# Router products in pairs on the halves of PE's columns, the second chunk's rows loaded later, and other numbers of buffers

## The chip, the cores and the metric

The kernel runs on one core of one Trainium2 chip. The metric is the device time of one execution in microseconds; the engines are named PE (matrix products, with PEld for its weight loads), DVE (vector), ACT (scalar activations), POOL (GpSimd) and SP (which here only issues transfers). 1607.1 us is the median of three runs (1601.46 to 1607.68).

## The reference, cut to what matters

```
h  = rmsnorm(x, g_mix) * (1 + sc1) + sh1            # x: 2048 tokens x 1024; sh, sc, gates from silu(c) @ ada_w
u  = a * sigmoid(gt),  [a, gt] = h @ w_in + b_in     # 1024 -> 2 x 1024
y  = causal depthwise conv of u, 31 taps, + b_dw
y  = silu(layernorm(y)) @ w_out
x  = x + g1 * y                                      # called x1 in the kernel
h  = rmsnorm(x, g_ffn) * (1 + sc2) + sh2
group = argmax(h @ w_rg + b_rg) of 4; the two best of the group's 8 experts by h @ w_re + b_re
x  = x + g2 * sum over the two of gate * ((silu(h @ w_gate[e]) * (h @ w_up[e])) @ w_down[e])
out = rmsnorm(x, g_final)
```

The router's weights are 4 + 32 = 36 columns. All is float32 at the interface; the large products are made of three products of split numbers (high x high, high x low, low x high).

## The kernel before, in words

The convolution half works on four chunks of 512 tokens (`c` 0 to 3) and, in each, on eight slices of 128 channels (`j` 0 to 7). A main loop over `s = 8 c + j` (L821) writes down, for each step, `conv_in` (two products of 24 matmuls each into `pg` and `pa`, then the gate, then the store of `u`, L410), with a lag of one step `dw` (the 31 taps, shared among PE, DVE and an ACT-and-POOL pair, L465), and for the chunk before `layer_norm` (L502), `conv_out` (L542) and, after its eighth slice, `finish` and `routing`. `PACE` says how many slices of `conv_out` go with a step. The conditioning products (`mod_pair`, L293) are spread over the first twenty steps by `MODS`. After the convolution, experts run in the written-out `ORDER`, from about 800 us on.

The order of each engine's queue is not the order of the text: the framework orders instructions by priority and by a timeline that it works out at build time. `urgent()` raises the priority of what stands in it, and `issue_after(i)` adds that the block's instructions on the engine of `i` stand behind `i` in that engine's queue. Each engine then works through its queue strictly in order, and waits where an operand or a buffer's place isn't there yet.

Places that the change touches:

- `conv_out` for one slice `j`: 24 matmuls into `po` (L388 to L390), `x1 = po * g1 + x` on DVE (L552), four transposes of `x1` (L555), their copy to `xr` (L557, L559), and the router product (L561): `x1` against 64 columns of router weights (36 of them used), even `j` on columns 0 to 63 of PE and on the first half of bank `lg`, odd `j` on columns 64 to 127 and on the second half. [...]
- `x1` tiles: a ring of `TMPB["x1"]` = 2 places; the rows' sums of squares (`junk`, L336) and `finish` use the same ring.
- `w` tiles of 512 KB: a ring of `WPB` = 8 places, used in pairs by every `w_unit` (high and low part of a weight) and by `mod_pair` (two blocks of `ada`).
- `modr` (L305): the result of a conditioning pair on its way from ACT back to PE (L308). The first eight pairs use the ring `prod` of 3 places, the 16 later ones a place of their own, `mp`. `prod` is also the ring through which ACT's tap products (L478) reach POOL's sums (L482, L484).
- `prep_load(c + 1)` at `j == 4` loads the next chunk's 512 rows (2 MB); for `c + 1 == 1` it is one transfer that stands in SP's queue behind the store of `u` of step `XSA` = 1 (L321). `prep_norm(c + 1)` at `j == 5` squares and scales the rows (L336, L342); `prep_tr` at `j == 7` transposes them (L357).

```
g = 64 * (j % 2)
nc.tensor.matmul(lg[g:g + 64, :n], wr2[:, j, :], x1[:, :n], start=(j < 2), stop=(j >= KD - 2),
                 tile_position=(0, g))
```

Of the kernel before, what the change touches and what calls it, by code (L numbers as in the profile page):

```python
# [9 lines left out]
F32 = mybir.dt.float32  # L10
# [11 lines left out]
P = 128  # L22
T = 2048
D = 1024
KD = D // P
# [8 lines left out]
N = [512, 512, 512, 512]  # L34
# [5 lines left out]
T0 = [sum(N[:c]) for c in range(NCH)]  # L40
TPC = [n // P for n in N]
# [31 lines left out]
LASTU = 600  # L73

LATER = {0: 1, 1: 1, 2: 1}
TABS, XSA, WPRI, ALT = 9, 1, 1000, 2
FIRST = (6,)

MODS = [0, 0, 1, 0, 1, 1, 1, 1, 1, 1, 1, 0, 1, 1, 1, 1, 1, 1, 1, 1]
# [15 lines left out]
MAXQ = max(q for t in TAPS for q, _ in t)  # L95
RW = CH + 4 * (MAXQ - 1)
WPB, WRB, UPB = 8, 1, 4
TMPB = {"acc2": 2, "prod": 3, "x1": 2}
BANKS = {"po": 1, "pa": 1, "pg": 1, "tr": 2, "lg": 1, "acc": 1, "out": 1}
LAG_DW, LAG_LN, LAG_OUT = 1, 2, 3  # L100
DELAY = 1
# [27 lines left out]
def moe_kernel(ctx, tc, x, xT, cols, ada, fing, w_in, w_out, b_r, wgu, wd, out):  # L129
    nc = tc.nc  # L130
# [27 lines left out]
    def col(name):  # L158
        a, b = COLS[name]
        return colt[:, a:b]  # L160
# [46 lines left out]
    def pool(name, bufs=1, stack=None, **kw):  # L207
        return (stack or p1).enter_context(tc.tile_pool(name=name, bufs=bufs, reuse_waits="tile", **kw))
# [6 lines left out]
    grp = [pool("grp1")]  # L215
    sp = {tag: pool("sp_" + tag, n) for tag, n in TMPB.items() if tag != "x1"}
    rt4 = pool("rt4")
# [5 lines left out]
    zp = pool("zp", KD)  # L223

    sp["x1"] = pool("sp_x1", TMPB["x1"])
    mp = pool("mp")
    right = ExitStack()
    wr = pool("wr", WRB, right, side="right")
    rp = pool("rp", RPB, right, side="right")
# [4 lines left out]
    wr2 = c1.tile([P, KD, 64], F32, name="wr2")  # L234
# [13 lines left out]
    def urgent(offset=URGENT):  # L248
        return tc.high_priority(offset=offset)

    def group(name, slot):
        return grp[slot].tile([P, 4, D], F32, tag="grp", name=name)

    def bank(tag, name):
        return ps[tag].tile([P, 512], F32, tag=tag, name=name)

    def tmp(tag, name, shape=(P, 512), dt=F32):
        return sp[tag].tile(list(shape), dt, tag=tag, name=name)
# [22 lines left out]
    def mod_rows(n):  # L281

        if n < KD // 2:
            return [raw("adar", True)[:] for _ in range(2)]
        if n < KD - 2:
            if n == KD // 2:
                adag.append(group("adag", 1))
            return [adag[0][:, 2 * (n - KD // 2) + i, :] for i in range(2)]
        return [wp.tile([P, D], F32, tag="w", name="adar")[:] for _ in range(2)]
# [3 lines left out]
    def mod_pair(bs, early=None):  # L293

        with urgent():
            rs = [wp.tile([P, D], F32, tag="w", name="adar")[:] for _ in bs] if early is None else mod_rows(early)
            for b, r in zip(bs, rs):
                nc.sync.dma_start(r, ada[b])
            pb = bank("out" if early is None else ("out", "acc", "lg", "po")[early % 4], "mod")
            for i, r in enumerate(rs):  # L300
                for k in range(KD):
                    g = 32 * (k % 4)
                    nc.tensor.matmul(pb[g:g + 32, i * P:(i + 1) * P], ca[:, k, :], r[:, k * P:(k + 1) * P],
                                     start=(k < 4), stop=(k >= 4), tile_position=(0, g))
            mr = mp.tile([P, 2, P], F32, tag="modr", name="modr") if early is None else tmp("prod", "modr", (P, 2, P))  # L305
            S.activation(mr[:], pb[:, :2 * P].rearrange("p (i q) -> p i q", q=P), AF.Copy)
            for i, b in enumerate(bs):
                nc.tensor.matmul(pb[:, 2 * P + i:2 * P + i + 1], mr[:, i, :], sel[:], start=True, stop=True)  # L308
            if bs[1] == bs[0] + 1:
                V.tensor_tensor(modc[:, bs[0]:bs[0] + 2], pb[:, 2 * P:2 * P + 2], col("adab")[:, bs[0]:bs[0] + 2], op=OP.add)  # L310
            else:
                for i, b in enumerate(bs):
                    V.tensor_tensor(modc[:, b:b + 1], pb[:, 2 * P + i:2 * P + i + 1], col("adab")[:, b:b + 1], op=OP.add)
# [3 lines left out]
    def prep_load(c):  # L317
        xs = group("xs", c == 1)
        t0 = T0[c] // P
        if c == 1:  # L320
            with tc.issue_after(u_stores[XSA].ins):  # L321
                nc.sync.dma_start(xs[:, :TPC[c], :], x[T0[c]:T0[c] + N[c], :].rearrange("(i p) d -> p i d", p=P))
        elif c == 0:
            for i in range(TPC[c]):
                nc.sync.dma_start(xs[:, i, :], x[(t0 + i) * P:(t0 + i + 1) * P, :])
        else:
            nc.sync.dma_start(xs[:, :TPC[c], :], x[T0[c]:T0[c] + N[c], :].rearrange("(i p) d -> p i d", p=P))
        return xs
# [15 lines left out]
    def parts(a):  # L344
        return a.rearrange("p (i q) -> p i q", q=P)
# [189 lines left out]
    def conv_out_tiles(c, o, n):  # L535
# [3 lines left out]
            xr = group("xr", 1)[:, :n // P, :]  # L539
        return xr, bank("lg" if o == 0 else "acc", "lg")  # L540

    def conv_out(c, o, n, j, z, xr, lg):  # L542

        end = c == NCH - 1
        w = wlast[j] if end else w_unit(c, w_out[j], (wo_d[0, j], wo_d[1, j]))
        x1 = tmp(X1E if end else "x1", "x1")
        with urgent(X1P):
            nc.sync.dma_start(x1[:, :n], xT[j][:, T0[c] + o:T0[c] + o + n])
        po = bank("pa" if end and j % 2 else "po", "po")
        gemm(po, w, z, n)  # L550
        with urgent():
            V.scalar_tensor_tensor(x1[:, :n], po[:, :n], modc[:, 16 + j:17 + j], x1[:, :n], op0=OP.mult, op1=OP.add)  # L552
            pb = bank("pg" if end and j % 2 else "out", "x1_t")
            for i in range(n // P):
                nc.tensor.transpose(pb[:, i * P:(i + 1) * P], x1[:, i * P:(i + 1) * P], ident[:])  # L555
            if j < XRV[c]:
                V.tensor_copy(xr[:, :, j * P:(j + 1) * P], parts(pb[:, :n]))  # L557
            else:
                S.activation(xr[:, :, j * P:(j + 1) * P], parts(pb[:, :n]), AF.Copy)  # L559
            g = 64 * (j % 2)  # L560
            nc.tensor.matmul(lg[g:g + 64, :n], wr2[:, j, :], x1[:, :n], start=(j < 2), stop=(j >= KD - 2),  # L561
                             tile_position=(0, g))

    def finish(c, o, n, xr, lg):

# [172 lines left out]
    early = {}  # L738
# [45 lines left out]
    with urgent(2 * URGENT):  # L784
        xs = prep_load(0)
# [13 lines left out]
    def begin(piece):  # L799
        c, o, n = piece  # L800
        zs[piece] = layer_norm(c, o, n, [ys[c * KD + k] for k in range(KD)])
        outs[piece] = conv_out_tiles(c, o, n)
# [10 lines left out]
    def parts_at(s):  # L813

        c, j = divmod(s - LAG_OUT, KD)
        if not 1 <= c < NCH:
            return []
        n = [sum(PACE[c - 1][:i]) for i in (j, j + 1)]
        return [(c - 1, q) for q in range(*n)]

    for s in range(NS + LAG_OUT):  # L821
        c, j = divmod(s, KD)
        if s < NS:
            us[s] = conv_in(c, j)
            if c + 1 < NCH:
                if j == 4:
                    xs = prep_load(c + 1)
                if s == TABS:
                    with tc.issue_after(u_stores[s].ins):
                        table_end[0] = nc.sync.dma_start(  # L830
                            tab_d[:].rearrange("(e o b) c -> o e (b c)", o=P, b=NRB),
                            ini[:].rearrange("p b c -> p (b c)")[:, None, :].to_broadcast([P, E, NRB * 3])).ins
                if j == 5:
                    prep_norm(c + 1, xs)
                if j == KD - 1:
                    for k in range(KD):
                        prep_tr(c + 1, xs, k)
        for t in (range(s - LAG_DW, s - LAG_DW + 1) if s < NS else range(max(s - LAG_DW, 0), NS) if s == NS else ()):
            if 0 <= t < NS:
                ys[t] = dw(t // KD, t % KD, us[t])  # L840
        cl, jl = divmod(s - LAG_LN, KD)
        if 1 <= cl < NCH and jl == 0:
            begin(PIECES[cl - 1])
        for co, jo in parts_at(s):
            ends.append((s + DELAY, part(PIECES[co], jo)))
        while ends and (ends[0][0] <= s or s == NS + LAG_OUT - 1):
            f = ends.pop(0)[1]
            if f:
                with urgent(ROUTE[done]):
                    f()  # L850
                done += 1
                if done == FIRST_AFTER:
                    first_expert()
        for _ in range(MODS[s] if s < len(MODS) else 0):
            if mods:
                mod_pair((mods.pop(0), mods.pop(0)))
                if len(mods) == 16:
                    mod_A2()
                if len(mods) == 8:
                    with urgent():  # L860
                        mod_end()
                if not mods:
                    mod_g2()
# [6 lines left out]
    for m in g2t:  # L870
        w, n = P // m, D // m
# [478 lines left out]
```

## Time and profile before

| | |
|---|---|
| median of three runs | 1607.1 us |
| the profiled execution | 1602.93 us |
| its span, first to last instruction | 1601.2 us |
| mean granted TensorE clock | 0.965 |
| PE busy | 1469.0 us, 92% |
| DVE busy | 1120.2 us, 70% |
| ACT busy | 973.9 us, 61% |
| POOL busy | 741.2 us, 46% |
| moved by the transfers | 456 MB, mean 285 GB/s |

The profile is of one execution. Times within it count from its first instruction. A busy time is the sum over a stretch, so an engine at 50 of 50 us never stood idle there. Idle time stands in brackets behind the instruction that ended it, with the engine or transfer that it waited for. The chain that ended last is followed back from the last instruction, from each piece to what released it.

### The profile page before, as it was taken

How to read it: one execution, taken by the hardware profiler on the slowest of the kernel's cores; microseconds unless marked ns; L12 is line 12 of the kernel's file. 1: busy time of each engine (PE TensorE's matmuls, PEld its weight loads, DVE VectorE, ACT ScalarE, POOL GpSimd, SP SyncE). 2: the span in 40 equal slices, each digit the busy share in tenths (PEclk: the TensorE clock that was granted, in tenths of full speed). 3: DMA queues.
4: the chain of work that ended last, by engine and by line, in shares of the span. 5: the costliest groups of instructions: out<-in, count | busy, mean ns of one | idle time of the engine just before them, and what ended most of it. 6: DMA issues, size and time to landing. Idle time of an engine off the chain costs nothing.

```text
span 1601.2 us, 24058 instructions
## 1 busy us (share of the span) xinstructions
PE 1469.0 (92%) x8269; PEld 1067.6 (67%) x8269; DVE 1120.2 (70%) x1779; ACT 973.9 (61%) x1600; POOL 741.2 (46%) x564
## 2 busy tenths in 40 slices
PE   5989998999999999969887899998999999999984
PEld 4766676677777776648663465565778676866763
DVE  2659987788998898874462447334579787898465
ACT  4676788877868794444420435324477677876453
POOL 0378898887689977823241112122122222232322
PEclk8999999899999999979999999999999999999988
DMA  9699898666776665672649989989899889998987
GB/s 356 256 336 331 252 296 297 218 227 247 289 276 214 210 242 212 212 280 84 240 152 289 398 291 345 338 306 362 280 378 331 282 304 364 358 335 270 365 288 280
DMA packets 123647, 455.99 MB, mean 285 GB/s; under 512 B 25594, under 2 KB 29058, under 8 KB 98946
## 3 DMA queue, kind: packets, MB, share of 16 engines
q1 hardware_dynamic: 93842, 362.48, 62.9%
q0 software_dynamic: 14224, 40.43, 9.8%
q10 hardware_dynamic: 15456, 51.51, 8.2%
q8 instruction: 66, 1.08, 0.3%
q14 instruction: 59, 0.48, 0.1%
HBM read 374.24 MB, written 80.13 MB: 284 GB/s over the span
## 4 chain that ended last, share of the span: by engine, by line
PE 65%; DMA 14%; DVE 11%; issue 4%; ACT 4%; POOL 2%; SPq 1%; ACTq 0%; POOLq 0%; DVEq 0%
PE pg L1111 15%; PE pd L1111 8%; PE pg L1113 5%; DVE acc L490 4%; PE po L388 3%; PE po L389 3%; PE po L390 3%; PE pg L388 3%; PE pa L388 3%; PE pa L389 3%; PE pa L390 3%; PE pg L390 3%; PE pg L389 3%; DMA wraw<-in_wgu 2%; PE lg L561 2%
## 5 line engine op out<-in xcount | busy, mean ns | idle before, releaser
L484 POOL TENSOR_TENSOR acc<-acc,prod 128x512 f32<-128x512 f32 x321 | 430.4, 1341 | 52.3 <-ACT prod L478 30.8
L490 DVE SCALAR_TENSOR_TENSOR acc<-u,colt,acc 128x512 f32<-128x512 f32 x497 | 369.5, 750 | 21.8 <-PE acc L461 13.0
L1035 DVE TENSOR_TENSOR wl<-wraw,wh 128x1024 fp32r<-128x1024 f32 x260 | 308.0, 1227 | 74.3 <-ACT wh L1034 68.9
L478 ACT ACTIVATE prod<-u,colt 128x512 f32<-128x512 f32 x385 | 269.3, 721 | 109.3 <-POOL acc L484 83.3
L1034 ACT ACTIVATE wh<-wraw 128x1024 fp32r<-128x1024 f32 x264 | 264.0, 1057 | 108.1 <-PE pd L1111 46.1
L1111 PE MATMUL pg<-wh,xh 128*128 128x512 f32 x464 | 152.5, 401 | 10.0 <-issue 6.9
L1156 POOL DMA_INDIRECT x2acc<-ys,ft x24 | 64.1, 2671 | 195.4 <-DVE ys L1153 189.9
L1111 PE MATMUL pg<-wh,xl 128*128 128x512 f32 x464 | 149.4, 396 | 0.0
L1111 PE MATMUL pg<-wl,xh 128*128 128x512 f32 x464 | 148.7, 395 | 0.1
L1113 PE MATMUL pg<-wraw,xh 128*32 128x256 f32 (+1 forms) x992 | 124.0, 462 | 4.2 <-DMA wraw<-in_wgu 3.7
L388 PE MATMUL pg<-hh,wh 128*128 128x512 f32 x256 | 105.1, 411 | 20.6 <-ACT u L420 9.9
L1156 POOL DMA_INDIRECT x2acc<-ys,rt x20 | 33.7, 1685 | 184.0 <-DVE ys L1153 104.0
L1111 PEld LDWEIGHTS pg<-wh,xh 128*128 128x128 f32 x464 | 87.2, 190 | 33.0 <-issue 10.2
L1129 ACT ACTIVATE sg<-pg 128x256 f32<-128x256 f32 (+1 forms) x79 | 26.7, 369 | 129.9 <-PE pg L1113 74.4
L1080 ACT ACTIVATE psx<-psx,modc,A 128x128 f32<-128x128 f32 x232 | 89.4, 438 | 26.4 <-issue 15.7
L390 PE MATMUL pg<-hh,wl 128*128 128x512 f32 x256 | 104.0, 406 | 1.5 <-DMA wl<-wi_d 1.5
L389 PE MATMUL pg<-hl,wh 128*128 128x512 f32 x256 | 104.3, 407 | 0.7 <-DVE hl L350 0.7
L388 PE MATMUL pa<-hh,wh 128*128 128x512 f32 x256 | 101.4, 396 | 1.2 <-DVE u L425 0.6
L1111 PEld LDWEIGHTS pg<-wl,xh 128*128 128x128 f32 x464 | 87.8, 190 | 20.1 <-DVE wl L1035 0.9
L390 PE MATMUL pa<-hh,wl 128*128 128x512 f32 x256 | 101.1, 395 | 0.0
L389 PE MATMUL pa<-hl,wh 128*128 128x512 f32 x256 | 101.2, 395 | 0.0
L388 PE MATMUL po<-zz,wh 128*128 128x512 f32 (+1 forms) x256 | 96.3, 381 | 4.9 <-ACT zz L349 4.9
(279 smaller groups left out, 2888.3 us busy)
## 6 DMA issues: line engine op xcount, KB each, us to landing
wraw<-in_wgu SPq DMA_DIRECT2D x128, 1024.0 KB, 8.8
wraw<-in_wd SPq DMA_DIRECT2D x64, 1024.0 KB, 7.6
adar<-in_ada SPq DMA_DIRECT2D x44, 512.0 KB, 9.7
wh<-wi_d SPq DMA_DIRECT2D x42, 512.0 KB, 4.7
wl<-wi_d SPq DMA_DIRECT2D x42, 512.0 KB, 5.9
wraw<-in_w_in SPq DMA_DIRECT2D x22, 512.0 KB, 8.5
wh<-wo_d SPq DMA_DIRECT2D x20, 512.0 KB, 4.5
wl<-wo_d SPq DMA_DIRECT2D x20, 512.0 KB
```

Of the source, the lines that this page charges most:

```text
L388: nc.tensor.matmul(po[:, :n], wh, xh[:, :n], start=(k == 0), stop=False)
L389: nc.tensor.matmul(po[:, :n], wh, xl[:, :n], start=False, stop=False)
L390: nc.tensor.matmul(po[:, :n], wl, xh[:, :n], start=False, stop=(k == KD - 1))
L478: S.activation(pr[:, :n], u[:, k:k + n], AF.Copy, scale=wdw[:, k:k + 1])
L484: Q.tensor_tensor(acc2[:, :n], acc2[:, :n], pr[:, :n], op=OP.add)
L490: V.scalar_tensor_tensor(acc, u[:, k:k + n], wdw[:, k:k + 1], acc, op0=OP.mult, op1=OP.add)
L1034: S.activation(h[:, o], r[:, o], AF.Copy)
L1035: (Q if len(ws) == 1 and n % 3 == 2 else V).tensor_tensor(l[:, o], r[:, o], h[:, o].bitcast(F32), op=OP.subtract)
L1080: S.activation(ps[:, q, :], ps[:, q, :], AF.Identity, bias=modc[:, 24 + k:25 + k], scale=A2[:, k:k + 1])
L1111: nc.tensor.matmul(outs[o][:], st[x], mv, start=a, stop=z)
L1113: nc.tensor.matmul(outs[0][o * w:(o + 1) * w, :n], st[x], mv, start=a, stop=z, tile_position=(0, o * w))
L1156: d = Q.indirect_dma_start(out=x2acc[:].rearrange("t (m n) -> (t m) n", m=s.m), out_offset=bass.IndirectOffsetOnAxis(ap=s.si, axis=0), in_ ...
```

## The change

The router products of chunks 0 to 2 are no longer issued slice by slice: the one of an even slice is held back, and after the following odd slice both are issued, the odd one first and the even one behind it. In chunk 3 nothing of this changes. Chunk 1's rows are loaded in four transfers of 512 KB instead of one of 2 MB, behind the store of step 4 instead of step 1, and their load and norm stand at `j` 6 and 7 instead of 4 and 5 (for chunks 2 and 3 they stay at 4 and 5). The ring of weights has nine places, that of `x1` four; the later `modr` go through `prod`, and `mp` is gone.

```
-TABS, XSA, WPRI, ALT = 9, 1, 1000, 2
+TABS, XSA, WPRI, ALT = 9, 4, 1000, 2
+NEXT_ROWS = [(6, 7), (4, 5), (4, 5)]
...
-WPB, WRB, UPB = 8, 1, 4
-TMPB = {"acc2": 2, "prod": 3, "x1": 2}
+WPB, WRB, UPB = 9, 1, 4
+TMPB = {"acc2": 2, "prod": 3, "x1": 4}
...
-    mp = pool("mp")
...
-            mr = mp.tile([P, 2, P], F32, tag="modr", name="modr") if early is None else tmp("prod", "modr", (P, 2, P))
+            mr = tmp("prod", "modr", (P, 2, P))
...
             with tc.issue_after(u_stores[XSA].ins):
-                nc.sync.dma_start(xs[:, :TPC[c], :], x[T0[c]:T0[c] + N[c], :].rearrange("(i p) d -> p i d", p=P))
+                for i in range(TPC[c]):
+                    nc.sync.dma_start(xs[:, i, :], x[(t0 + i) * P:(t0 + i + 1) * P, :])
...
-            g = 64 * (j % 2)
-            nc.tensor.matmul(lg[g:g + 64, :n], wr2[:, j, :], x1[:, :n], start=(j < 2), stop=(j >= KD - 2),
-                             tile_position=(0, g))
+            routed[j] = x1
+            def product(q):
+                g = 64 * (q % 2)
+                return nc.tensor.matmul(lg[g:g + 64, :n], wr2[:, q, :], routed.pop(q)[:, :n], start=(q < 2), stop=(q >= KD - 2),
+                                        tile_position=(0, g))
+            if end:
+                product(j)
+            elif j % 2:
+                with tc.issue_after(product(j).ins):
+                    product(j - 1)
...
-                if j == 4:
+                if j == NEXT_ROWS[c][0]:
                     xs = prep_load(c + 1)
...
-                if j == 5:
+                if j == NEXT_ROWS[c][1]:
                     prep_norm(c + 1, xs)
```

## Rows read from the trace of the kernel before

**Rows 1.** The page's first part: the span, and the busy time of each engine.
```profile
span 1601.2 us, 24058 instructions
PE 1469.0 (92%) x8269; PEld 1067.6 (67%) x8269; DVE 1120.2 (70%) x1779; ACT 973.9 (61%) x1600; POOL 741.2 (46%) x564
```

**Rows 2.** Busy time by stretch where `conv_out` runs. Columns: the stretch, its length, busy us of PE, PEld, DVE, ACT and POOL (instructions), granted clock, busy share of the transfer engines, GB/s. The last row is a stretch of the experts.
```profile
290.00:420.00 130.00, 128.12 (x757) 96.91 (x756) 108.88 (x164) 97.83 (x161) 107.77 (x84) 1.00 0.65 227
420.00:480.00 60.00, 57.74 (x333) 44.92 (x332) 59.19 (x121) 44.30 (x76) 44.72 (x35) 1.00 0.83 307
480.00:580.00 100.00, 100.00 (x464) 77.24 (x464) 89.27 (x137) 80.83 (x131) 92.14 (x74) 1.00 0.58 199
610.00:705.00 95.00, 87.30 (x388) 60.03 (x387) 80.81 (x127) 39.21 (x60) 63.63 (x53) 0.96 0.66 227
1300.00:1400.00 100.00, 96.61 (x587) 75.88 (x588) 79.08 (x91) 77.58 (x126) 24.46 (x15) 0.98 0.97 353
```

**Rows 3.** The router products: their group over the whole execution (busy us, mean ns of one, idle before), and from PE's order of time one of them with what runs behind it. Columns of the latter: start, length, engine, line, what, how many.
```profile
L561 PE MATMUL lg<-x,wr 128*64 128x512 f32 x48 | 27.0, 645 | 0.5 <-DVE x L552 0.5
...
308.60 1.07 PE L561 MATMUL lg<-x,wr 128*64 128x512 f32 x2
309.60 0.50 PE L388 MATMUL po<-zz,wh 128*128 128x512 f32 x1
```

**Rows 4.** PE's order of time where products on the halves (128*64) and on the quarters (128*32) of the columns run in a row already, with what follows each.
```profile
932.21 5.36 PE L1113 MATMUL pg<-wraw,xh 128*64 128x512 f32 x22
937.51 0.66 PE L1136 MATMUL psh<-ident,sg 128*128 128x128 f32 x4
...
951.63 3.65 PE L1113 MATMUL pd<-wraw,hidh 128*64 128x512 f32 x16
955.22 0.74 PE L1111 MATMUL pg<-wl,xh 128*128 128x512 f32 x2
```

**Rows 5.** Pieces of the chain that ended last, in order of time: start, length, what.
```profile
73.12 14.09 DMA wraw<-in_w_in
89.73 2.08 ACT junk L336 x4
92.42 0.58 ACT u L420
93.04 0.80 PE pg L388
```

**Rows 6.** SP's queue in order of time around the rows of chunk 1, and (last line) the one long wait in it that a transfer of these rows ended: total us, times, longest.
```profile
69.39 0.33 SPq L426 DMA_DIRECT2D u_d<-u  x1
69.77 0.47 SPq L322 DMA_DIRECT2D xs<-in_x  x1
73.12 2.57 SPq L372 DMA_DIRECT2D wraw<-in_w_in  x2
77.08 9.81 SPq L457 DMA_DIRECT2D R<-u_d  x4
87.03 0.35 SPq L372 DMA_DIRECT2D wraw<-in_w_in  x1
112.81 0.33 SPq L426 DMA_DIRECT2D u_d<-u  x1
118.82 2.76 SPq L372 DMA_DIRECT2D wraw<-in_w_in  x2
143.45 0.33 SPq L426 DMA_DIRECT2D u_d<-u  x1
SPq L457 <- DMA xs<-in_x: 8.2, 1, 8.2
```

**Rows 7.** ACT's order of time: the wait for a weight, the first square of the rows, their scaling and what comes behind it; and the time that the one transfer of the rows took from issue to landing.
```profile
87.66 0.72 ACT L478 ACTIVATE prod<-u,colt 128x512 f32<-128x512 f32 x1 [8.29 <-DMA wraw<-in_w_in]
89.63 1.04 ACT L336 ACTIVATE junk<-xs 128x1024 bf16<-128x1024 f32 x1
99.67 4.26 ACT L342 ACTIVATE xs<-xs,rs 128x1024 f32<-128x1024 f32 x4
103.83 0.22 ACT L428 ACTIVATE halo<-u 128x30 f32<-128x30 f32 x1
DMA to landing us min/median/max: 11.0/11.0/11.0
```

**Rows 8.** PE's order of time: its idle times in chunk 0 after 60 us, and the first transposes of chunk 1's rows.
```profile
93.04 0.80 PE L388 MATMUL pg<-hh,wh 128*128 128x512 f32 x1 [5.70 <-ACT u L420]
127.35 0.50 PE L388 MATMUL pg<-hh,wh 128*128 128x512 f32 x1 [1.99 <-ACT u L420]
142.75 0.50 PE L388 MATMUL pg<-hh,wh 128*128 128x512 f32 x1 [1.86 <-ACT u L420]
157.40 0.66 PE L357 MATMUL xT<-ident,xs 128*128 128x128 f32 x4
```

**Rows 9.** Busy time by stretch in chunk 0, columns as in rows 2.
```profile
95.00:105.00 10.00, 10.00 (x38) 8.12 (x37) 2.96 (x3) 10.00 (x16) 7.99 (x7) 0.82 1.02 394
115.00:125.00 10.00, 10.00 (x79) 7.26 (x83) 9.27 (x11) 5.97 (x10) 8.98 (x7) 1.00 1.03 350
```

**Rows 10.** The longest idle time of PE between 95 and 600 us (two lines of its order of time).
```profile
282.32 0.76 PE L388 MATMUL pg<-hh,wh 128*128 128x512 f32 x1 [6.21 <-DMA wh<-wi_d]
284.72 0.79 PE L390 MATMUL pg<-hh,wl 128*128 128x512 f32 x1 [1.21 <-DMA wl<-wi_d]
```

**Rows 11.** ACT's total wait for places of `prod` up to 750 us (us, times, longest), and the instructions that write `modr` (ns min/median/max, first and last start).
```profile
ACT prod L478 <- POOL acc L484: 83.3, 106, 8.4
L306 ACT ACTIVATE modr<-mod x24: 358/367/393, 15.0 to 464.7; 128x256 f32<-128x256 f32 x24
```

More of the change, by code (lines that the diff above doesn't have):

```diff
@@ L540, in conv_out_tiles @@
         return xr, bank("lg" if o == 0 else "acc", "lg")
+    routed = {}
     def conv_out(c, o, n, j, z, xr, lg):
```

## The prediction

> **What bounds the kernel now.** I read the page's busy shares first: PE works 92% of the span, no other engine over 70% [rows 1]. That is a mean over stages, so I went on to busy time by stretch. Where `conv_out` runs PE is busy 128.1 of 130, 57.7 of 60, 100.0 of 100 and 87.3 of 95 us; DVE comes close behind, and in 420 to 480 us it is ahead with 59.2 of 60 [rows 2]. So in the first and third of these stretches a microsecond less on PE can be a microsecond less of time; in the second DVE decides, in the last neither is full. The experts after them are PE's again (96.6 of 100 with the transfer engines at 0.97) and their own work isn't touched [rows 2]: what is won before them moves them as a whole. Third, the chain of waits in chunk 0: it goes through a weight's transfer of 14.1 us, then ACT's squares of the next rows, then ACT's `u`, and PE resumes at 93.04 after 5.70 us idle [rows 5, 8]. Fourth, SP's queue tells why: the 2 MB of rows go out at 69.77, the weights behind them at 73.12, and the next transfers stand 8.2 us until the rows have landed [rows 6].
>
> **The products, step by step.** Chunks 0 to 2 have 24 router products, each two instructions, 48 in all. One product starts at 308.60 and the next matmul at 309.60: 1.00 us of PE [rows 3]. What a pair costs is not in the trace at this line, but two other places show products on both halves in a row: 22 instructions take from 932.21 to 937.51, which is 0.24 us each and 0.96 for four, and 16 take 3.59 us, 0.90 for four [rows 4]. Four instructions are one pair of products. So a pair costs what one product alone costs, and 12 pairs save 12 x 1.0 = 12 us of PE at most; at least nothing, if something stands between the two. Of this I count by stretch. Chunk 0's four pairs lie in 290 to 420 us, PE 98.5% busy: 3 of 4 us, the rest held by DVE's full stretch behind it. Chunk 1's lie mainly in 480 to 580, PE without a gap and DVE with 10.7 us to spare: 3.5 of 4. Chunk 2's lie in 610 to 705, where PE has 7.7 us idle as it is: 1.5 of 4 [rows 2]. Sum **-8**, bounds -12 and 0. The last pair of a chunk ends no later than the single product did, so `finish` isn't held back.
>
> The Trainium skill speaks against the full saving: "TensorE: Matmul & The Clock Gate", section on packing small matmuls, gives three column tiles as 2.38 times as fast, 0.79 of the ideal. By that a pair would be estimated at 1.26 of a product, 12 pairs would save 8.9 us instead of 12, and the whole sum below would be about -9 instead of -11. The rows show no such loss at this shape (0.90 to 0.96 against 1.00), and I go by them.
>
> The held-back slice keeps its `x1` for one more slice; with four places two can be held and two loaded ahead, as one and one before. I price this at 0: 0.5 us of idle stood before the products in all [rows 3].
>
> **The rows of chunk 1.** Without the 2 MB at 69.77, SP is not held for 8.2 us and the weights of 73.12 don't share the engines with them. ACT waits 8.29 us for that weight, then does two squares, 2.08 us, before the `u` that PE wants [rows 5, 7]. Gain at most the 5.70 us of PE's idle time, since PE is full on both sides of it. Against that: the rows now go out after step 4's store (112.81 at the earliest) into a stretch where the engines are at 1.03 already and PE is full [rows 6, 9]. Four issues of 0.47 instead of one add 1.4 us to SP's queue. Two weights at 118.82 stand behind, and two idle times of 1.99 and 1.86 us follow [rows 6, 8]; they may grow. The norm's ACT work (from 89.63 to 103.83, 14.2 us with what is between) moves behind them, and must be done by 157.40, when the transposes begin [rows 7, 8]: 112.81 + 11.0 + 14.2 = 138.0, 19 us ahead. I take **-3**, about half of the 5.70, because the transfer is moved and not removed; bounds -6 and +4 (the two idle times doubled).
>
> The skill's "DMA: Bandwidth & Descriptors", section Bandwidth, asks for transfers of at least 1 MiB for three quarters of the peak, which speaks against splitting the rows. The trace has the one 2 MB transfer landing in 11.0 us and blocking what stands behind it; by the page the four together would land later than that, the gain of this term would fall towards 0 and the sum to -8. No row shows that loss, and I keep -3.
>
> **Nine weights.** Tiles are taken in pairs from a ring, so a ninth place lets one of the two parts start one unit earlier, the other not. PE's longest idle time is such a wait, 6.21 us for the high part and 1.21 for the low [rows 10]. With the high part already there, the low one is alone on the way; the third matmul wants it. I take **-1**; bounds -4 (half of the 7.4 us) and 0.
>
> **`modr` through `prod`.** Sixteen tiles now take one of three places which ACT already waits for 106 times, 83.3 us in all, 0.79 on average [rows 11]. 16 x 0.79 = 12.6 us of ACT waiting at worst, in stretches where PE has other work in its queue; PE waits only if its L308 comes too soon. I take **+1**, bounds 0 and +4.
>
> **Sum:** -8 - 3 - 1 + 1 = -11 us; the bounds add to -22 and +8. The profiled execution took 1602.93 us (span 1601.2 and 1.7 around it), so the sum is 1592; the median is 4.2 us higher, and from it the same sum gives 1596. I take the middle, **1594**.
>
> **Rivals.**
> 1. *DVE takes over.* PE's saving becomes waits for DVE and POOL, which are at 84 to 99% and 67 to 92% in these stretches [rows 2]; the pairs give 3 us instead of 8. For it: the stretch of 420 to 480 us. Against it: 480 to 580, where only PE is full. Then -6 at most and about -5 with no gain from the weights: 1600.
> 2. *The change doesn't do what it says.* The even product only has to stand behind the odd one, not next to it; urgent transposes can be placed between, and then each costs its own 1.00 us. The pairs give 0 and the sum is -3: 1602. Against it: nothing is gained for the planner by parting two products that are ready together.
> 3. *Slower: the rows come too late.* If the planner lets them out only at the step-6 store (143.45), they are ready at 143.45 + 11.0 + 14.2 = 168.7, 11.3 us after PE wants them [rows 6 to 8]. The norm then falls into the full boundary stretch and costs up to its four squares and scalings, some 9.5 us of ACT, from the chain; and PE's clock, which after the idle time at 93 us was granted at 0.82 for ten us, costs 1.8 more [rows 9]. Together 22.6, less the 5.7 saved and the 8 of the pairs: +9, and from the same middle (1605) 1614. It decides when the last of the four lands after 157.4 - 14.2 = 143.2. Against it: `issue_after` alone allowed the rows out 0.4 us after the named store before [rows 6], though the call stood at `j == 4`.
>
> **Chances.** About 0.5% (8 us) is what a measurement of this kernel can tell from no change. The forecast has 0.52, and nearly all of it is faster by more than that. DVE taking over has 0.23 and unpaired products 0.10; both are within 0.5%. Late rows have 0.15: mostly slower, a little of it within. So faster 0.51, same 0.36, slower 0.13. The forecast's own range is 1584 to 1600 (pairs at 11 or at 5, rows at -6 or +2). To leave out no more than two in ten, the range reaches down to 1582 and up to 1609, into rivals 1 and 2 wholly and into a part of 3.
>
> **What would show it.** Right: L561 appears as x4 with about 1.0 us to the next matmul, 12 times; the idle time before 93 us is gone, and SP's queue shows no 8-us wait behind the rows; the stretch from the first `po` matmul to the last router product of chunk 2 is about 8 us shorter; first transposes of chunk 1 come 3 to 6 us earlier, not later. Wrong: L561 as x2 twice (rival 2); x4, but new idle times of PE before L555 or L527 with DVE as the releaser (rival 1); an idle time before L357 with ACT `xs` as the releaser (rival 3); PE idle before L308 with ACT `modr` (the term of +1 too small). I would be wrong altogether if the build-time planner, given other places, put the chunks in a different order on the engines, so that the time moved where none of these four terms is.

## The result, and the profile after

The changed kernel takes 1626.06 us (median of four runs, 1624.39 to 1627.54); the kernel before took 1604.28 us beside it. The ratio is 1.0149 [1.0122 to 1.0176]: slower by 1.5%, or 22 us between the medians, where 11 us less had been forecast. It lies above the whole range. The page's head first; its rows answer to [rows 1].

```profile
span 1625.8 us, 24056 instructions
...
PE 1465.0 (90%) x8269; PEld 1076.4 (66%) x8269; DVE 1123.8 (69%) x1779; ACT 973.8 (60%) x1600; POOL 748.9 (46%) x564
```

The work is the same: PE has 4 us less of it, DVE, ACT and POOL at most 7.7 us more, the weight loads 8.8. So the 24.6 us of longer span are mostly waiting, on every engine. The mean granted clock is 0.954 instead of 0.965; it is lower where PE stands idle more (0.92 against 0.96 in 610 to 705 us) and goes along with the waits. Where they arise is read from the windows that answer to [rows 2].

```profile
290.00:420.00 130.00, 125.33 (x744) 96.22 (x744) 107.50 (x160) 93.76 (x154) 99.83 (x77) 0.97 0.65 227
420.00:480.00 60.00, 55.05 (x332) 44.77 (x331) 50.70 (x106) 42.75 (x72) 34.75 (x28) 1.00 0.92 338
480.00:580.00 100.00, 100.00 (x476) 79.87 (x475) 83.69 (x121) 72.95 (x121) 91.36 (x72) 1.00 0.60 202
610.00:705.00 95.00, 83.95 (x383) 60.85 (x383) 83.41 (x135) 54.33 (x85) 81.64 (x66) 0.92 0.54 186
```

The column to look at is the last engine's. POOL did 107.8 us of work in the first stretch and 44.7 in the second; now it does 99.8 and 34.8. Some 18 us of its work are pushed back, and in 610 to 705 it does 18 us more (81.6 against 63.6). The chain that ended last shows the same in 640 to 720 us. Columns: start, length, what; the changed kernel first, then the kernel before.

```profile
664.47 4.86 DMA tab_d<-ent,hi
...
671.15 1.30 POOL acc L486
672.53 1.28 POOL acc L486
...
676.44 1.35 ACT prod L480 x2
...
703.64 1.30 POOL acc L486
704.96 0.73 ACT prod L480
711.88 0.75 DVE x L556
```
```profile
669.58 6.01 DMA R<-u_d
675.73 2.73 PE acc L461 x18
...
688.64 0.73 DVE x L552
689.38 5.94 DVE acc L490 x9
...
700.25 1.91 PE lg L561 x2
```

Before, the end of chunk 2 hung on PE and DVE. Now it hangs on 23 of POOL's tap sums of some 1.29 us each, almost back to back from 671 to 705, behind a run of POOL's routing-table writes (`tab_d`) with a transfer of 4.86 us between them. The last router product of chunk 2 starts at 713.3 instead of 700.2 us, the last of all at 815.9 instead of 794.3. From there to the end it is 809.9 against 806.9 us: 21.6 of the 24.6 us are lost before the experts.

Two of the four parts show as forecast. PE's order of time has all twelve pairs as one group of four instructions; this is the first (compare [rows 3]):

```profile
315.18 1.08 PE L568 MATMUL lg<-x,wr 128*64 128x512 f32 x4
316.19 0.50 PE L392 MATMUL pa<-hh,wl 128*128 128x512 f32 x1
```

From 315.18 to 316.19 is 1.01 us for two products, where one took 1.00. Ten of the twelve groups give 1.01; the one at 695.85, behind 2.98 us of idle PE, takes 1.91 at a granted clock of 0.50, the lower of its two levels, as the single product at 700.25 did before at 0.50; behind the last one PE stands idle. And SP's queue (compare [rows 6]) lets the four loads of chunk 1's rows out in a row, with the next weight behind them and no 8-us wait:

```profile
110.69 0.34 SPq L428 DMA_DIRECT2D u_d<-u  x1
111.07 5.72 SPq L324 DMA_DIRECT2D xs<-in_x  x4
118.56 0.33 SPq L374 DMA_DIRECT2D wraw<-in_w_in  x1
```

The idle time of PE before 93 us [rows 8] is gone. In its place stand three shorter or later ones (PE's order of time, 60 to 160 us):

```profile
122.77 0.79 PE L390 MATMUL pg<-hh,wh 128*128 128x512 f32 x1 [6.47 <-ACT u L422]
...
154.56 0.50 PE L390 MATMUL pg<-hh,wh 128*128 128x512 f32 x1 [1.18 <-ACT hh L351]
156.08 0.63 PE L359 MATMUL xT<-ident,xs 128*128 128x128 f32 x4 [1.02 <-DVE hl L352]
```

**Where POOL loses its time.** POOL sums what ACT writes into `prod`. This is POOL's order of time around the end of chunk 0, with its largest wait, and ACT's order in the same stretch:

```profile
422.94 1.02 POOL L269 TENSOR_TENSOR rs<-ms,mhalf 128x4 f32<-128x4 f32 x1 [3.60 <-DVE ms L268]
435.88 1.30 POOL L484 TENSOR_TENSOR acc<-prod 128x512 f32<-128x512 f32 x1 [11.93 <-ACT prod L480]
```
```profile
416.32 0.73 ACT L480 ACTIVATE prod<-u,colt 128x512 f32<-128x512 f32 x1
...
421.49 1.07 ACT L589 ACTIVATE junk<-xr 128x1024 bf16<-128x1024 f32 x1
...
427.76 2.18 ACT L601 ACTIVATE xr<-xr,rs 128x1024 f32<-128x1024 f32 x2
...
434.20 0.38 ACT L307 ACTIVATE modr<-mod 128x256 f32<-128x256 f32 x1 [0.40 <-ACT xr L601]
434.48 1.33 ACT L480 ACTIVATE prod<-u,colt 128x512 f32<-128x512 f32 x2
```

For 18.2 us, from start to start, ACT writes no tap product. It does the squares and scalings of `finish`, and the next tap product comes 0.28 us after a `modr`. In the kernel before ACT does the same squares and scalings (L577, L589), but tap products stand between them, and the `modr` comes after:

```profile
420.42 0.72 ACT L478 ACTIVATE prod<-u,colt 128x512 f32<-128x512 f32 x1
...
422.07 1.33 ACT L478 ACTIVATE prod<-u,colt 128x512 f32<-128x512 f32 x2
...
427.82 1.34 ACT L478 ACTIVATE prod<-u,colt 128x512 f32<-128x512 f32 x2
...
434.92 1.96 ACT L478 ACTIVATE prod<-u,colt 128x512 f32<-128x512 f32 x3
436.76 0.39 ACT L306 ACTIVATE modr<-mod 128x256 f32<-128x256 f32 x1
```

I counted, over ACT's whole queue, how many tap products stand before each `modr`, against the text. Before, all 16 later `modr` stand elsewhere than in the text: nine of them 12 to 30 tap products earlier, seven 3 to 25 later. In the changed kernel none of 24 is out of the text's order. Tap products and `modr` now take places of one ring, and ACT's queue keeps them in the order in which the text takes those places. So the taps of the next slice wait behind a `modr`, and `modr` behind PE's conditioning product and the scalings that the queue has set ahead of it. That this is why the build-time planner left them in order is inferred from the queues; no profile shows a planner.

What the order costs here can be read off. The tap products that begin at 434.48 belong to slice (2,2), that is `j` = 2 of chunk 2, counted by the tap products ahead of them. DVE had finished that slice's `u`, their operand, at 392.6; POOL had worked off the slice before at 419.3; the conditioning product that the `modr` reads ended only at 430.6 (orders of time of DVE, POOL and PE, in this order):

```profile
391.91 0.69 DVE L427 SCALAR_TENSOR_TENSOR u<-u,pa 128x512 f32<-128x512 f32 x1
407.08 12.26 POOL L486 TENSOR_TENSOR acc<-acc,prod 128x512 f32<-128x512 f32 x9
429.55 1.08 PE L304 MATMUL mod<-adar,ca 128*32 128x128 f32 x32
```

### The profile page after: what moved, and what is told of

It is laid out like the page before. It is cut to its first block, busy times and chain, and to the rows that moved or that the text cites. A ratio compares the mean times of both kernels' runs of the same rounds, so it can differ in the third digit from the quotient of the medians.

```text
span 1625.8 us, 24056 instructions
## 1 busy us (share of the span) xinstructions
PE 1465.0 (90%) x8269; PEld 1076.4 (66%) x8269; DVE 1123.8 (69%) x1779; ACT 973.8 (60%) x1600; POOL 748.9 (46%) x564
## 4 chain that ended last, share of the span: by engine, by line
PE 56%; DMA 14%; DVE 12%; ACT 6%; POOL 6%; issue 5%; SPq 1%; ACTq 0%; POOLq 0%; DVEq 0%
PE pg L1123 15%; PE pd L1123 8%; PE pg L1125 5%; POOL acc L486 5%; DVE acc L492 4%; DMA wraw<-in_wgu 3%; PE po L390 3%; PE po L391 3%; PE po L392 2%; PE pg L390 2%; DMA wraw<-in_wd 2%; PE pg L392 2%; PE pa L392 2%; PE pg L391 2%; PE pa L390 2%
## 5 line engine op out<-in xcount | busy, mean ns | idle before, releaser
L1123 PEld LDWEIGHTS pg<-wh,xl 128*128 128x128 f32 x464 | 87.6, 190 | 18.7 <-DVE xl L1107 0.8
```

What stands on the lines that cost most here:

```text
L1123: nc.tensor.matmul(outs[o][:], st[x], mv, start=a, stop=z)
```

## Experiments

The theory (A): the new order of `modr` and taps in `prod` holds POOL up and costs more than the whole change. Rivals: (B) the ninth weight place, (C) the rows, (D) with faster products, POOL's taps become the bound by themselves. The expectations call A theory M, B theory W, C theory R; their theory O is that any edit makes the planner draw all queues anew, and that this alone costs. The ratios below are to the kernel before on the same chip, whose median was 1601.3 to 1603.2 us.

**The parts one by one.** Into the kernel before: the pairs with four `x1` places; `modr` in `prod`; the rows with their four loads, step and `XSA`; nine weight places.

```
b_pairs:  "x1": 2 -> 4, product(j), product(j - 1) as in the change
b_modr:   mr = tmp("prod", "modr", (P, 2, P)), mp gone
b_rows:   XSA 1 -> 4, NEXT_ROWS, four loads of 512 KB
b_w9:     WPB 8 -> 9
```

> The kernel before with only the products in pairs and the x1 ring at four (weights 8, rows and modr as before). After the change POOL's sums of the taps fall behind by 27 us between 210 and 470 us, waiting for ACT's tap products, and everything behind the second chunk is late by that. Theory M (modr through prod starves POOL): this kernel has no such loss and keeps the pairs' gain, 1592 to 1600. Theory R (the rows at the first chunk boundary): the same, 1592 to 1600. Theory O (any edit makes the build-time planner order ACT's and POOL's queues anew, and the loss is in the order and not in a part): no telling from the part; POOL idle for ACT's products in 210 to 480 us decides the time, 26 us more of it gives 1620 or more.

> The kernel before with only the late modr tiles through the ring prod instead of a place of their own. Theory M: 1615 to 1630, POOL's y of chunk 2 late by 15 us or more, with waits of ACT's products for PE's L308 or of modr for PE's L303. Theory R: 1602 to 1606. Theory O: no telling; the time goes with POOL's idle time in 210 to 480 us (36 us before, about 62 after).

> The kernel before with only the second chunk's rows later (behind the store of step 4, four transfers, load and norm at j 6 and 7). Theory R: step (1,0) comes 5 to 10 us later than before though chunk 0 ends 5 to 9 us earlier, and the total is 1610 to 1625. Theory M: 1598 to 1604. Theory O: no telling from the part; as above.

> The kernel before with only nine places for the weights. Theories M and R: 1598 to 1605, the 7.4 us of PE idle near 282 us shorter by 1 to 4. Theory O: can be off by 10 us or more in either direction, with POOL's idle time for ACT's products.

| kernel | us | ratio to before |
|---|---|---|
| `b_pairs` | 1600.80 | 0.9994 [0.9978 to 1.0011] |
| `b_modr` | 1620.87 | 1.0121 [1.0096 to 1.0145] |
| `b_rows` | 1606.86 | 1.0036 [1.0018 to 1.0053] |
| `b_w9` | 1615.51 | 1.0086 [1.0057 to 1.0115] |

No part alone is faster, and `modr` alone costs 19 us. It shows the same two marks, in ACT's and in POOL's order of time:

```profile
411.27 0.72 ACT L477 ACTIVATE prod<-u,colt 128x512 f32<-128x512 f32 x1 [0.27 <-POOL acc L483]
...
437.93 0.39 ACT L305 ACTIVATE modr<-mod 128x256 f32<-128x256 f32 x1 [3.84 <-PE mod L302]
438.21 1.32 ACT L477 ACTIVATE prod<-u,colt 128x512 f32<-128x512 f32 x2
```
```profile
439.61 1.29 POOL L481 TENSOR_TENSOR acc<-prod 128x512 f32<-128x512 f32 x1 [12.97 <-ACT prod L477]
```

Here 26.9 us without a tap product, and `modr` waits by name for PE's conditioning product. B isn't refuted either: nine weights alone cost 13 us. One change shows in SP's queue. Low and high part of a weight, issued 0.42 us apart before (272.97 and 273.39 us), come 9.9 us apart:

```profile
278.63 0.37 SPq L379 DMA_DIRECT2D wh<-wi_d  x1
...
288.52 0.39 SPq L380 DMA_DIRECT2D wl<-wi_d  x1
```

PE stands 9.92 us for the low part at 297.41; before it stood 6.21 and 1.21 [rows 10]. With nine places and tiles taken in pairs, some pairs straddle the ring's end, and the two places come free apart; that this parts the two issues is inferred from the code and these times. PE's wait is 2.5 us longer by it, of a loss of 13. From 95 to 600 us PE stands idle for 29.5 us instead of 18.2; in that, 5.21 are for a `modr` and 3.66 for conditioning weights, and what makes those late was not followed.

**Out of the whole change.** `modr` with its own place again, `x1` three; the change with eight weights; both at once (`x1` four); and both with `x1` three.

```
a_mp:     mp = pool("mp") and its line kept; "x1": 3
a_w8:     WPB = 8
a_mp8:    mp kept, WPB = 8   (pairs, rows, four x1 are left)
a_mp8x3:  as a_mp8, "x1": 3
```

> The changed kernel with modr in a place of its own again (x1 at three places instead of four, for room). Alone on the kernel before, modr through prod cost 1.2%, with the same late POOL chain as the whole change (sums of the taps late by 28 us from slice 5 of chunk 2). Theory M (modr's place in the ring holds back ACT's tap products until PE's conditioning product is done): most of that comes back, 1604 to 1612, no gap of 10 us or more in ACT's tap products around 420 to 435 us. Theory O (only the order drawn anew, no part to blame): as likely as not still 1615 to 1630.

> The changed kernel with eight places for the weights again. Nine alone cost 0.9% on the kernel before, with PE idle 9.9 us for low parts. Theory W (with an odd number of places the low and the high part of one weight are released apart, and the low part comes late): 1610 to 1618 and PE idle for low parts under 2 us in 210 to 300 us. If the late POOL chain decides alone (theory M): 1622 to 1628, as with nine.

> The changed kernel with modr in its own place and eight places for the weights: what is left of the change is the pairs, x1 at four and the later rows. With nine it came out at 0.9965. Theory W (nine places cost 0.9 to 1.0% wherever they stand): 1583 to 1591. If nine only hurt together with modr through prod: 1594 to 1602.

> As a_mp (modr in its own place, pairs, rows, x1 at three places), with eight weights instead of nine. a_mp gave 0.9965; with eight weights and x1 at four it was 0.9899. If nine weights are what costs the 0.7%: 0.985 to 0.992, 1578 to 1590. If it is the place of x1: 0.994 to 0.999, 1593 to 1600.

| kernel | us | ratio to before |
|---|---|---|
| `a_mp` | 1597.55 | 0.9965 [0.9942 to 0.9987] |
| `a_w8` | 1608.55 | 1.0046 [1.0020 to 1.0071] |
| `a_mp8` | 1587.28 | 0.9899 [0.9854 to 0.9943] |
| `a_mp8x3` | 1593.19 | 0.9950 [0.9920 to 0.9980] |

With `modr` out of `prod` the change is faster: between the changed kernel and `a_mp` lie 1.84% (the `x1` places differ too, three for four), between `a_w8` and `a_mp8`, where nothing else differs, 1.47%. `a_mp8` beats both kernels; its last router product starts at 781.7 us, 12.6 earlier than before. Its ACT writes tap products between the squares and the scalings again, and right behind the scalings, with no `modr` ahead of them:

```profile
420.69 1.33 ACT L480 ACTIVATE prod<-u,colt 128x512 f32<-128x512 f32 x2
...
428.67 1.33 ACT L480 ACTIVATE prod<-u,colt 128x512 f32<-128x512 f32 x2
429.89 0.72 ACT L480 ACTIVATE prod<-u,colt 128x512 f32<-128x512 f32 x1
...
431.07 0.39 ACT L307 ACTIVATE modr<-mod 128x256 f32<-128x256 f32 x1
```

The waits of POOL for tap products from 210 to 480 us give the same in sum (us, times, longest), first the changed kernel, then `a_mp8`; before it was 11.8 and 10.1.

```profile
POOL acc L484 <- ACT prod L480: 26.5, 9, 11.9
POOL acc L486 <- ACT prod L480: 17.7, 13, 4.4
```
```profile
POOL acc L486 <- ACT prod L480: 15.3, 11, 4.8
...
POOL acc L484 <- ACT prod L480: 2.1, 2, 1.3
```

The first sum of each slice, as start in POOL's order of time less the same start before, follows one pattern (us):

| slice (chunk, `j`) | after | `b_modr` | `a_w8` | `a_mp` | `a_mp8` | `b_pairs` | `b_w9` |
|---|---|---|---|---|---|---|---|
| (2,1) | +22.8 | +17.2 | +7.7 | +6.3 | 0.0 | +2.5 | +17.0 |
| (2,2) | +34.1 | +37.8 | +21.5 | +3.2 | +0.2 | +2.3 | +13.6 |
| (2,3) | +46.1 | +50.4 | +35.1 | +6.3 | -0.8 | +6.9 | +14.5 |
| (2,5) | +27.2 | +28.7 | +13.1 | +2.1 | -3.9 | +3.0 | +15.8 |

The two jumps of 11 to 21 us at (2,2) and (2,3) stand in all kernels with `modr` in `prod` (in the two of the next part as well), and in none of the others. `b_w9` is late too, but by a step that came earlier. The jumps aren't the whole loss, nor do they last in full: POOL makes good 19 of the changed kernel's 46.1 us by (2,5). Of the 17.0 us that part `a_w8` from `a_mp8` there, 7.7 stood at (2,1) already; how those arose was not followed.

**More places, or less waiting?** If taken places were the cost, as the prediction priced it, a fourth place of `prod` should bring it back. If order is, it should not, and an earlier or later `modr` should matter instead. `a_mods2` takes the last eight conditioning pairs two steps later.

```
b_modr_p4:  b_modr, "prod": 3 -> 4
a_mods2:    MODS = [0, 0, 1, 0, 1, 1, 1, 1, 1, 1, 1, 0, 0, 0, 1, 1, 1, 1, 1, 1, 1, 1]
```

> The kernel before with the late modr through prod, and prod with four places instead of three. Theory M by number of places: a fourth place gives back what modr takes, 1598 to 1608. Theory M by order (a tap product that stands behind modr in ring and queue waits for it whatever the number of places): 1612 to 1625. Without modr in it a fourth place would do little, as POOL takes the products one after the other.

> The changed kernel with the last eight conditioning pairs two steps later in the text, nothing else; modr still goes through prod. In the plan before, the later modr stand up to 24 tap products behind their place in the text; in the changed one modr and tap products stand in ACT's queue strictly in the order of the text. Theory M by order: with the text's place nearer to where modr can be had, ACT's gap in tap products around 420 us shrinks and POOL's chain is less late, 1605 to 1615. If the mere presence of modr in the ring costs (places taken): 1620 to 1628.

`b_modr_p4` took 1628.30 us, 1.0153 [1.0116 to 1.0190]: no better than with three places. POOL's wait is still there:

```profile
441.28 1.30 POOL L481 TENSOR_TENSOR acc<-prod 128x512 f32<-128x512 f32 x1 [12.09 <-ACT prod L477]
```

So it is not the number of places. The order was the same: in `b_modr_p4`, and in every other kernel here with `modr` in `prod`, no `modr` left the text's order among the tap products. `a_mods2` took 1611.20 us, 1.0054 [1.0035 to 1.0073]: 0.95 of the 1.49% are back, but not in the way expected. ACT's stretch without a tap product did not shrink (408.58 to 428.41), and it still ends right behind a `modr`:

```profile
408.58 0.73 ACT L479 ACTIVATE prod<-u,colt 128x512 f32<-128x512 f32 x1 [0.26 <-POOL acc L485]
...
428.14 0.39 ACT L306 ACTIVATE modr<-mod 128x256 f32<-128x256 f32 x1
428.41 1.34 ACT L479 ACTIVATE prod<-u,colt 128x512 f32<-128x512 f32 x2
```

POOL's wait there is 6.95 instead of 11.93 us, yet (2,5) is still 24.7 us late. The total agrees with A, the path doesn't; this run supports A in part only, and how late sums cost less here stays open.

**Is it POOL by itself?** Rival D was tried by relieving POOL in two ways: slices 0 to 5 of chunk 2 give taps of POOL to PE, in `b_pairs`; and the last taps are left out.

```
b_pt6:  b_pairs, TAPS[2] = [(1, 16)] * 6 + [(0, 18)] * 2
b_lt:   cut = 2 if c in (1, 2) else 0; range(t1, W - cut), range(t0, t1 - cut)
b_plt:  b_lt and b_pairs
```

> The kernel before with products in pairs, x1 at four, and in slices 0 to 5 of chunk 2 four taps given from DVE and POOL to PE (two of 18 on DVE, two of 13 on ACT and POOL, one row of quarters on PE, 1.0 us each). Pairs alone came out at 0.9994, with y of the slices 2 to 5 us late. Theory D (DVE and POOL set the pace once PE has 12 us less): the 6 us on PE are free, DVE loses 9 and POOL about 10 us, 1585 to 1596. If PE still sets the pace: 1603 to 1610.

> The kernel before with four taps fewer in each slice of chunks 1 and 2 (two on DVE, two on ACT and POOL, 16 slices; that part of the convolution is left out). It frees 1.5 us of DVE and 2.7 us of POOL per slice. Theory D (DVE and POOL set the pace between 300 and 600 us as much as PE): 10 to 25 us less, 1578 to 1593. If PE alone set it: 1598 to 1604.

> The same with four taps fewer in each slice of chunks 1 and 2, and the products in pairs with x1 at four. Theory D: with DVE and POOL out of the way the pairs' 12 us on PE become time, 6 to 12 us less than the same without pairs. If the pairs' saving is lost to something else (order, `finish`, waits for x1): no more than 3 us apart.

`b_pt6` took 1622.03 us, 1.0103 [1.0060 to 1.0146]: by the ratios 1.09%, some 17 us, slower than `b_pairs`. So these taps moved to PE are no relief; what they cost there was not followed further. `b_lt` took 1701.45 (1.0616 [1.0583 to 1.0648]) and `b_plt` 1693.83 (1.0571 [1.0542 to 1.0601]). Both are some 100 us longer than the full kernel, though their convolutions end earlier: the last router product of all starts at 791.3 and 789.7 us, 794.3 before. All of the loss lies in the experts (909.8 us from that product to the end in `b_lt`, 806.9 before). Both have 120 matmul instructions more than the kernel before (8389 for 8269), which fits that left-out taps change the data by which tokens are routed. So these totals tell nothing against the kernel before. Against each other, pairs with four `x1` places are worth 7.6 us (0.45%, with intervals that overlap) with four taps less in each slice, where the same edit to the full kernel, `b_pairs`, gave 0.06%. That is inside the 6 to 12 us expected if D holds; but only 1.6 us of it stand at the end of the convolution in the profiled runs. D is neither shown nor refuted.

**The fourth place of `x1`, and the rows with it.**

```
b_x1:       "x1": 2 -> 4
b_rows_x1:  b_rows and b_x1
```

> The kernel before with x1 at four places and nothing else. The prediction priced it at 0. If x1's places, and not the pairs, are what makes the later rows pay (b_rows alone 1.0036, with pairs and x1 0.9899): 1590 to 1598. If they do nothing: 1599 to 1604. If they cost the 8 us that the pairs alone did not show (b_pairs 0.9994): 1608 to 1614.

> The kernel before with the later rows and x1 at four places, without pairs. With pairs as well it was 0.9899, rows alone 1.0036. If the pairs are worth their 8 to 12 us of PE here: 1595 to 1602. If x1's places made the difference and the pairs nothing: 1585 to 1590.

`b_x1` took 1611.10 us, 1.0053 [1.0027 to 1.0078]; `b_rows_x1` 1602.85, 1.0002 [0.9975 to 1.0028]. Two more places of a buffer, which no product uses for anything new, cost 0.5%. By differences of medians' ratios:

| part | alone | in company |
|---|---|---|
| pairs | | -0.59% (`b_pairs` less `b_x1`), -1.03% (`a_mp8` less `b_rows_x1`) |
| rows | +0.36% | -0.51% (`b_rows_x1` less `b_x1`), -0.95% (`a_mp8` less `b_pairs`) |
| nine weights | +0.86% | +1.03% (after less `a_w8`), +0.15% (`a_mp` less `a_mp8x3`) |
| `modr` in `prod` | +1.21% | +1.47% (`a_w8` less `a_mp8`) |
| four `x1` | +0.53% (for two) | -0.51% (for three; `a_mp8` less `a_mp8x3`) |

Each difference has an interval of some 0.3 to 0.5% to either side, so the signs of `modr` and of the pairs are firm; those of nine weights with `mp` kept and of `x1` in company are not. Theory O stays as a part of it: `b_x1` shows that new queues alone can cost 0.5%. `modr` in `prod` costs more than twice that, both times, with the same jumps.

Of the totals, those of `b_modr`, `a_mods2`, `a_mp8`, `a_mp8x3` and `b_x1` lie in a range that had been expected; `b_pairs` and `b_rows_x1` miss one by less than 1 us. `b_rows`, `b_w9`, `b_modr_p4`, `b_pt6` and `b_lt` are slower than the ranges they were to be read by, `a_mp` and `a_w8` faster.

## Why the prediction was wrong, point by point

- **`modr` through `prod`, +1 with bounds 0 and +4: the step that failed.** It read the ring as a matter of places: 16 tiles by 0.79 us, "12.6 us of ACT waiting at worst" [rows 11]. Four places instead of three brought nothing back. What went with the shared ring in every kernel was a fixed order: taps behind a `modr` that waits for a transfer and for PE. It costs 1.2 to 1.5%, 19 to 24 us, five to six times the upper bound. The sign that I named, PE idle for ACT's `modr`, was the wrong place to look: in the changed kernel no such wait is over 0.31 us (`b_modr` has one of 5.65, `a_w8` one of 8.74), while POOL stands 11.93 us for tap products. POOL was out of my sum, although it is at 92.1 of 100 us in 480 to 580 [rows 2], where the 27 us that it is late at (2,5) stay as they are.
- **Nine weights, -1 with bounds -4 and 0: wrong in sign.** +13 us alone. That a ninth place serves one part of a pair was seen; that it parts the two, so that PE waits for the later, was taken for a gain. But that wait is not the whole price: in `a_mp` PE stands 9.3 us for one low part too, in `a_mp8x3`, with eight places, 9.1 for one high part, and nine weights cost 0.15% between these two, within the interval.
- **`x1` at 0: the term was missing.** Alone it costs 0.53%, 8 us. That it gives the planner other queues to draw is inferred, and which of them costs is not shown; a price of 0 would have needed bounds to both sides.
- **Pairs, -8: right in the mechanism.** 1.01 us for two, and -0.59 to -1.03%, some 9 to 16 us, as differences between kernels that both have four `x1` places; `b_pairs` itself is level with the kernel before. The upper end is more than the 12 us of PE's own work, so some of it is again other queues. The estimate from the three-tile figure in the Trainium skill's "TensorE: Matmul & The Clock Gate", section on packing small matmuls, was 1.26 products for a pair; the trace shows 1.01 at this shape.
- **Rows, -3 with bounds -6 and +4: bounds too narrow on both sides.** The 8.2-us wait and the 5.70 us of idle are gone; but 6.47 us of idle at 122.77 stand where 1.99 stood at 127.35 [rows 8], one of the "two idle times" that I let double. By `b_rows` the part costs 0.36%, about 6 us (3 to 8 by its interval); in company it gains 0.51 or 0.95%, about 8 or 15. Landing in time for the norm was right: rival 3's idle time before the transposes is 1.02 us, and DVE ends it, not ACT's rows. They start 13.6 us earlier than before (143.80 for 157.40), not 3 to 6, and yet the first `po` matmul comes 10.5 us later (258.61 for 248.15).
- **Rivals.** None of the three is what happened. Rival 2 is refuted by twelve groups of four. Rival 1 named DVE, with POOL beside it: it is POOL that takes over, and not for the pairs' sake. The stretch from the first `po` matmul to the last router product of chunk 2, which was to be about 8 us shorter, is 454.7 us instead of 452.0; in `a_mp8` it is 435.9. The last sentence of the prediction, other orders of the queues through other places, is what came; it stood there without a price and without a chance. The four runs of parts sum to +2.4%, where 1.5% was measured: they don't add, and no run tells how the rest is shared.

**What stays open.** Why the rows pay only with four `x1` places, why nine weights cost nothing when `modr` has its own place, and how `a_mods2` gets back 15 us with POOL's sums still late (up to its last router product the granted clock is 0.97, in the changed kernel 0.95). Each of these kernels has its own queues, and one profile of each doesn't separate an edit from the plan that came with it.

## What to carry to other kernels

A ring that two streams share makes one order of them: keep a tile that waits for a long chain (transfer, PE, ACT) out of the ring of a dense producer and consumer, and ask for the order before the number of places. An odd number of places for tiles that are taken in pairs is worth a run of its own: here nine cost 0.9% alone, 1.0% with `modr` in `prod`, and nothing that can be told from 0 where `modr` has its own place. Where queues are planned at build time, price a change of a buffer's number with bounds to both sides, and take a bundle of edits apart on the chip: here two parts of five ate what three had won, and without those two the kernel is 1.0% faster than before.

## What had not been expected of the hardware

Nothing. The pair's price, 1.01 us for two products of a 128x512 tile on either half of PE's columns where one took 1.00, had been forecast from two other places of the same trace.
